# Where a convolution keeps its running sum, who splits the gate weights, and when its layer norm is issued: the last layer of a two-layer diffusion backbone

## The chip, the cores and the metric

The kernel runs on one core of a Trainium2 chip. The metric is the device time of one execution in microseconds (us), as the median of three runs. Five engines with instruction queues of their own work side by side: TensorE (PE: matrix multiplications, written to PSUM), VectorE (DVE), ScalarE (ACT), GpSimd (POOL) and SyncE (SP, which here only issues DMA transfers). Each takes its instructions strictly in the order in which the program was built, and an instruction waits at the head of its queue for what it needs. L1205 is line 1205 of the kernel before; the lines of the changed kernel from L1199 on are one or two higher.

## The reference

Two layers over 512 latent tokens and 256 context tokens of width 1024. Each has a token-mixing part (a convolution branch and an attention branch, merged by gates) and an MLP. The last layer computes only the latent tokens' output; the context gives it just keys and values.

```python
def conformer_conv(u, w_dw, b_dw, ln_g, ln_b):      # u (B, L, 2*512)
    a, g = u[..., :512], u[..., 512:]
    z = a * sigmoid(g)
    z = conv_depthwise(z, w_dw, width=31, pad=15) + b_dw      # per channel, along the tokens
    return silu(layernorm(z, ln_g, ln_b))

def merge_branches(conv_in, attn, gate_logits, ...):
    y_conv = conformer_conv(conv_in, ...) @ w_conv_out        # 512 -> 1024
    y_attn = attn @ w_attn_out                                # 1024 -> 1024
    g = sigmoid(gate_logits + b_gate)                         # 2 * 1024
    return (g[..., :1024] * y_conv + g[..., 1024:] * y_attn) @ w_out

# layer:  p = modulate(rmsnorm(x)) @ w_in    (columns: conv | q | k | v | gates)
#         x = x + gate1 * merge_branches(p_conv, diff_attention(q, k, v), p_gates, ...)
#         x = x + gate2 * sqrelu_mlp(modulate(rmsnorm(x)), w1, w2)
```

## The kernel before

**Three-pass products.** Activations lie with channels on the 128 partitions and tokens along the free axis. A float32 factor is split into a high part, rounded on ACT (L76), and a low part, the remainder, by one subtraction on DVE or POOL (L80). `fm_block` then adds three matmuls for each 128x128 piece of weight and 512 tokens: high times high (L142), low activation times high weight (L143), high activation times low weight (L144). A block of 128 output columns over 1024 input channels is 24 such matmuls. `h_x`, `l_x` and `r_x` are the high part, low part and raw load of weight `x`; `h1h`, `h1l` those of the layer's input, and later, in the same buffers, those of the attention output.

**Stages of the last layer.** The eight attention heads run with projections beside them as filler, the last of them the convolution's input (`z`, L749). Then, in the order of the program:

- The **gate loop**: eight slabs of 256 columns, tiles `gt`, first the four of the attention gates (`half` 1, tiles `g_1_0` to `g_1_7`), then the four of the convolution gates (`half` 0). `gate_slab(half, s, engine)` loads and splits a slab; the low part goes to DVE where no engine is given. Of the 16 `gt` blocks each is 24 matmuls and a sigmoid on ACT (L1257). Slab (1,0) is loaded early and has its low part on POOL; (1,1) is loaded just ahead of the loop, on DVE.
- `spill_rstd`, called in the loop at slab (1,2): the attention heads' normalizing factors `rsall` take a power on POOL (L1028), are transposed on PE (`rsT`, L1058), copied (L1060) and written to memory. From there `branch_load` fetches attention output `ar` and factors `arb` for each head and multiplies them on DVE (L1232); eight heads, four of them loaded ahead.
- The **attention output**: eight blocks `ya`, two for each of four slabs of `w_attn_out`. It needs the splits `h1h`, `h1l` of all eight heads. DVE multiplies each finished block into its gate (`g`, L1335). `ya` has two PSUM banks ("mm"), so a block may start only when that product has read the block two before it.
- The **convolution output**: eight blocks `yc` over four channel tiles, from `ch` and `cl`, the high and low part of the convolution's result; then merge, output projection, second norm and MLP.

**The convolution** is a generator, `taps`: four channel tiles of 128x512, 31 taps each, one DVE instruction for each tap. The first (L1201) starts the sum with the bias, the others (L1205) multiply a shifted view of `z` by a per-channel weight and add the running sum, which lies in SBUF (`ca`, shown as `cacc`). The gate loop and the attention output draw on the generator by `some_taps(n)`: six taps after each of 16 gate blocks, seven after each `ya` block of the first two slabs; what is left is drained ahead of the layer norm.

**The layer norm** of the convolution is a generator of three parts, advanced by `next(ln, None)`. Part 1: the sum `tot` of the four channel tiles on DVE (L1276), a matmul with ones that gives all partitions the mean (`ln`, L1279), four subtractions on DVE (L1283), four squares on ACT and three additions on DVE (`vs`, L1290). Part 2: four small matmuls of `vs`, the reciprocal root on DVE and POOL (`ms_cv`, L354 and L355), its diagonal `dg_cv` (L361). Part 3: a matmul that spreads it over the partitions (L365), then scale (L1308), sigmoid and product (L1312) on DVE and ACT, which give `ch` and `cl`.

**Order.** A scheduler sets each engine's order when the program is built, by priorities that follow the program's order and by its own estimates; the queues are fixed from then on. PSUM has eight banks. In this stage two are "mm" (`gt` and `ya` alternate in them), four "mi" (`ln`, `rsT` and the like), and two "mc", which `ps_for` uses for the context tokens alone, so that the last layer leaves them empty.

Of the kernel before, what the change touches and what calls it, by code (L numbers as in the profile page):

```python
# [8 lines left out]
F32 = mybir.dt.float32  # L9
F32R = mybir.dt.float32r  # L10
AF = mybir.ActivationFunctionType
ALU = mybir.AluOpType
AX = mybir.AxisListType

P = 128
# [11 lines left out]
TAPS = 31  # L27
# [24 lines left out]
def trunk_kernel(  # L52
# [6 lines left out]
    nc = tc.nc  # L59
# [77 lines left out]
    def rows(src, col0, ncols):  # L137
        return src[:, col0 : col0 + ncols].rearrange("(k p) n -> p k n", p=P)
# [318 lines left out]
    for s in range(2):  # L457
        nc.vector.tensor_tensor(
            out=cvec[:, :, s], in0=L["cols"][:, R_C + 8 * s : R_C + 8 * s + 8],
            in1=sg[:, 8 * s : 8 * s + 8], op=ALU.mult)  # L460
# [224 lines left out]
    for i in range(DEPTH):  # L685
        last = i == DEPTH - 1
# [21 lines left out]
        zt = [None] * CT  # L708
# [48 lines left out]
        def gate_slab(half, s, lo_eng=None):  # L757
            wg[half, s] = load_slab(rows(wi, G_OFF + half * D + 256 * s, 256),
                                    f"wg{i}_{half}_{s}", lo_eng=lo_eng)
# [304 lines left out]
        def drain(gen):  # L1064
            for _ in gen:
                pass
# [110 lines left out]
        mc = mcp.__enter__()  # L1177
# [9 lines left out]
        def g3(name, dt=F32):  # L1187
            return gp.tile([P, NT], dt, tag="g3", name=name, bufs=16)
# [3 lines left out]
        CV = nv if last else SEQ + PAD + CTX  # L1192
        CA = qp.tile([P, CT, CV], F32, tag="qk", name=f"cacc{i}")
        ca = [CA[:, cc] for cc in range(CT)]

        def taps():
            for cc in range(CT):
                for t in range(TAPS):
                    wcol = wdc[:, t * CT + cc : t * CT + cc + 1]  # L1199
                    if t == 0:  # L1200
                        nc.vector.tensor_scalar(ca[cc][:, :CV], zt[cc][:, 0:CV], wcol,  # L1201
                                                cols[:, R_BDW + cc : R_BDW + cc + 1],
                                                ALU.mult, ALU.add)
                    else:
                        nc.vector.scalar_tensor_tensor(  # L1205
                            out=ca[cc][:, :CV], in0=zt[cc][:, t : t + CV], scalar=wcol,
                            in1=ca[cc][:, :CV], op0=ALU.mult, op1=ALU.add)
                    yield

        tap = taps()  # L1210

        per_gate, per_ya = (6, 7) if last else (7, 6)

        def some_taps(n):
            for _ in range(n):
# [22 lines left out]
        for half, lst in ((1, ga), (0, gc)):  # L1238
            for s in range(4):
                if (half, s) not in wg:  # L1240
                    gate_slab(half, s)
                if (half, s) == (1, 2):
                    drain(spill_rstd())
                if half == 0 and s == 3:
                    for hg in branch[:4]:
                        branch_load(*hg)
                w = wg.pop((half, s))
                for m in range(2):
                    mb = 2 * s + m
                    t = g3(f"g{i}_{half}_{mb}")  # L1250
                    lst[mb] = t
                    for g in groups:
                        W = g.stop - g.start
                        ps = ps_for(g, f"gt{i}_{half}_{mb}_{g.start}")
                        fm_block(ps[:, :W], w, m * P, lambda k: (hh[:, k], hl[:, k]), g)
                        bcol = R_BG + half * KT + mb
                        nc.scalar.activation(out=t[:, g], in_=ps[:, :W], func=AF.Sigmoid,  # L1257
                                             bias=cols[:, bcol : bcol + 1])
                    some_taps(per_gate)
                    if m == 0 and not state.get("ada_done"):  # L1260
                        ada_slab(i, L, 8 + 4 * half + s)
# [63 lines left out]
        for s in range(4):  # L1325
            w = load_slab(rows(w_attn_out[i], 256 * s, 256), f"wao{i}_{s}")
            if not state.get("ada_done"):
                ada_slab(i, L, 16 + s)
            for g in groups:
                W = g.stop - g.start  # L1330
                for m in range(2):
                    mb = 2 * s + m
                    ps = ps_for(g, f"ya{i}_{mb}_{g.start}")
                    fm_block(ps[:, :W], w, m * P, lambda k: (ah[:, k], al[:, k]), g)
                    nc.vector.tensor_tensor(out=ga[mb][:, g], in0=ga[mb][:, g], in1=ps[:, :W],  # L1335
                                            op=ALU.mult)
                    if last and (s, m) == (3, 0):
                        next(ln, None)
                if s < 1 + last:
                    some_taps(per_ya)  # L1340
            if s == last:
                drain(tap)
                ln = layer_norm()
            if s >= last:
                next(ln, None)


        CL = hpool.tile([P, KT, NT], F32R, tag="hl", name=f"cl{i}")
        for cc in range(CT):
            for a0, W, t0 in cgr:  # L1350
                low = nc.vector.tensor_tensor(out=CL[:, cc, t0 : t0 + W],
                                              in0=ca[cc][:, a0 : a0 + W],
                                              in1=f32(CH[:, cc, t0 : t0 + W]), op=ALU.subtract)
        normed.append(low.ins)
        mh, ml = [None] * KT, [None] * KT
        for s in range(2):
# [7 lines left out]
            for m in range(4):  # L1364
# [9 lines left out]
                for g in groups:  # L1374
                    rr[g.start] = gp.tile([P, 512], F32, tag="ar", bufs=3,
                                          name=f"mr{i}_{mb}_{g.start}")[:, : g.stop - g.start]
# [650 lines left out]
```

## Time and profile before

| | |
|---|---|
| median of 3 runs | 2313.78 us (2309.47 to 2314.64) |
| the profiled execution | 2309.04 us, its span 2307.3 us |
| PE busy | 2234.8 us, 97% of the span, 14402 matmuls |
| DVE busy | 1679.5 us, 73%, 2759 instructions |
| ACT busy | 1056.3 us, 46% |
| POOL busy | 625.9 us, 27%, 774 instructions |
| TensorE clock granted, mean | 0.993 |
| gate loop ends, attention output begins (PE) | 1836.5 us |
| last tap of the last layer's convolution begins (DVE) | 1852.0 us |
| first `yc` block begins (PE) | 1889.5 us |

A row of the timeline reads: start in us, duration, engine, line, operation, output and inputs by the program's names, shapes, count, and in brackets how long the engine was idle just before and what ended that. Rows of groups read: line, engine, operation, forms and count, then busy us, mean ns of one, and idle us before them. Rows of windows give for each stretch its length, the busy us of PE, of the weight loads, of DVE, ACT and POOL (with instructions), the granted clock, the DMA share and GB/s.

### The profile page before, as it was taken

What the parts mean: (1) busy time and instruction counts of PE and PEld (TensorE: products, weight loads), DVE (VectorE), ACT (ScalarE), POOL (GpSimd) and SP (SyncE); (2) the same over time, 40 slices, a digit from 0 to 9 for tenths busy, and PEclk for the clock granted to TensorE, in tenths of its full rate; (3) what the DMA queues carried; (4) which work ended last, traced back from release to release, by engine and by line L of the source; (5) the groups of instructions that cost most, each with busy time, mean ns of one, the idle gap of its engine ahead of it and who ended that gap; (6) DMA issues with size and microseconds to landing.
All of it is one profiled execution on the core that took longest, in us unless ns stands there. A gap on an engine that the chain in (4) does not pass through costs nothing.

```text
span 2307.3 us, 36445 instructions
## 1 busy us (share of the span) xinstructions
PE 2234.8 (97%) x14402; PEld 2021.1 (88%) x14402; DVE 1679.5 (73%) x2759; ACT 1056.3 (46%) x2049; POOL 625.9 (27%) x774
## 2 busy tenths in 40 slices
PE   8999999999999999999999998999999999999999
PEld 6999998888888989998899998999877779888887
DVE  6777776599657678787786567776849966757673
ACT  5555655422323264343346345555642333654541
POOL 1966765110000021222222256766611000100000
PEclk9999999999999999999999999999999999999999
DMA  9211111134444611333345422111114423443151
GB/s 310 62 35 45 47 47 45 44 124 151 148 140 152 203 50 52 105 110 100 128 133 164 141 71 58 44 45 44 43 62 144 130 76 112 154 128 99 66 183 37
DMA packets 202267, 232.63 MB, mean 101 GB/s; under 512 B 8864, under 2 KB 162928, under 8 KB 201968
## 3 DMA queue, kind: packets, MB, share of 16 engines
q1 hardware_dynamic: 202096, 230.30, 31.2%
q8 instruction: 113, 1.85, 0.3%
q14 instruction: 58, 0.48, 0.1%
HBM read 212.93 MB, written 17.35 MB: 100 GB/s over the span
## 4 chain that ended last, share of the span: by engine, by line
PE 75%; DVE 10%; POOL 5%; ACT 4%; DMA 3%; issue 2%; SPq 0%; DVEq 0%; POOLq 0%; ACTq 0%
PE r L151 4%; PE f L143 3%; PE f L144 3%; PE f L142 3%; PE r L143 3%; PE r L142 3%; PE r L144 3%; PE gt L142 3%; PE gt L143 3%; PE gt L144 3%; PE qk L142 2%; PE qk L143 2%; PE qk L144 2%; PE r L154 2%; PE yc L151 2%
## 5 line engine op out<-in xcount | busy, mean ns | idle before, releaser
L1205 DVE SCALAR_TENSOR_TENSOR cacc<-z,cols,cacc 128x783 f32<-128x783 f32 (+1 forms) x240 | 208.6, 929 | 0.3
L142 PE MATMUL qk<-h_wqk,h1h 128*128 128x256 f32 x640 | 182.6, 287 | 2.3 <-ACT rw L797 1.5
L143 PE MATMUL qk<-l_wqk,h1h 128*128 128x256 f32 x640 | 180.2, 284 | 0.0
L969 DVE TENSOR_REDUCE st<-S 128x1 f32<-128x768 f32 (+1 forms) x160 | 134.6, 846 | 57.6 <-PE S L967 56.3
L144 PE MATMUL qk<-h_wqk,h1l 128*128 128x256 f32 x640 | 176.4, 284 | 0.0
L972 ACT ACTIVATE e<-S,st 128x768 f32<-128x768 f32 (+1 forms) x160 | 131.2, 823 | 40.1 <-DVE st L969 39.8
L143 PE MATMUL f<-h2hl,h_w 128*128 128x512 f32 (+1 forms) x416 | 144.0, 347 | 1.2 <-POOL h2hl L80 1.1
L142 PE MATMUL f<-h2hh,h_w 128*128 128x512 f32 (+1 forms) x416 | 142.4, 348 | 2.1 <-ACT h2hh L387 1.1
L144 PE MATMUL f<-h2hh,l_w 128*128 128x512 f32 (+1 forms) x416 | 143.1, 345 | 0.0
L142 PE MATMUL gt<-h1h,h_wg 128*128 128x512 f32 (+1 forms) x384 | 138.1, 360 | 0.0
L143 PE MATMUL gt<-h1l,h_wg 128*128 128x512 f32 (+1 forms) x384 | 136.7, 356 | 0.0
L144 PE MATMUL gt<-h1h,l_wg 128*128 128x512 f32 (+1 forms) x384 | 136.5, 356 | 0.0
L151 PE MATMUL r<-F,whir 128*128 128x512 f32 (+1 forms) x384 | 124.8, 340 | 2.2 <-ACT F L1655 1.9
L142 PEld LDWEIGHTS qk<-h_wqk,h1h 128*128 128x128 f32 x640 | 122.2, 191 | 4.5 <-ACT rw L797 1.7
L151 PE MATMUL r<-F,wlor 128*128 128x512 f32 (+1 forms) x384 | 124.8, 340 | 0.5 <-POOL wlor L1573 0.2
L143 PEld LDWEIGHTS qk<-l_wqk,h1h 128*128 128x128 f32 x640 | 122.2, 191 | 0.3 <-POOL l_wqk L80 0.3
L144 PEld LDWEIGHTS qk<-h_wqk,h1l 128*128 128x128 f32 x640 | 119.9, 191 | 0.3 <-POOL h1l L80 0.2
L142 PE MATMUL v<-h_wv,h1h 128*128 128x256 f32 x384 | 112.2, 292 | 6.5 <-ACT rwc L861 4.0
L324 DVE SCALAR_TENSOR_TENSOR adaac<-ar,cvec,adaac 128x512 f32<-128x512 f32 x105 | 94.5, 919 | 30.7 <-DMA ar<-in_w_ada_dram 30.6
L144 PE MATMUL v<-h_wv,h1l 128*128 128x256 f32 x384 | 109.9, 286 | 0.0
L143 PE MATMUL v<-l_wv,h1h 128*128 128x256 f32 x384 | 109.3, 285 | 0.0
L803 POOL TENSOR_TENSOR rqk<-rqk,mhalf 128x4 f32<-128x4 f32 x80 | 85.8, 1075 | 78.7 <-DVE rqk L802 77.5
(400 smaller groups left out, 7453.5 us busy)
## 6 DMA issues: line engine op xcount, KB each, us to landing
r_w<-in_w_mlp_dram SPq DMA_DIRECT2D x34, 1024.0 KB, 5.4
ada<-in_w_ada_dram SPq DMA_DIRECT2D x24, 1024.0 KB, 5.4
ar<-in_w_ada_dram SPq DMA_DIRECT2D x96, 256.0 KB, 3.3
r_wg<-in_w_in_dram SPq DMA_DIRECT2D x16, 1024.0 KB, 5.2
r_wqk<-in_w_in_dram SPq DMA_DIRECT2D x30, 512.0 KB, 5.1
rf<-in_w_mlp_dram SPq DMA_DIRECT2D x26, 512.0 KB, 3.9
rr<-in_w_mlp_dram SPq DMA_DIRECT2D x24, 512.0 KB, 3.7
r_wao<-in_w_attn_out_dram SPq DMA_DIRECT2D x8, 1024.0 KB, 5.2
```

Source lines behind the costliest of these rows:

```text
L142: nc.tensor.matmul(ps, sh, mh, start=first, stop=False)
L143: nc.tensor.matmul(ps, sh, ml, start=False, stop=False)
L144: nc.tensor.matmul(ps, sl, mh, start=False, stop=last)
L151: nc.tensor.matmul(ps, w[j][:, k, m0 : m0 + P], a(k)[0][:, toks], start=k + j == 0, stop=False)
L154: nc.tensor.matmul(ps, w[0][:, k, m0 : m0 + P], a(k)[1][:, toks], start=False, stop=k == nk - 1)
L324: nc.vector.scalar_tensor_tensor(out=a, in0=r, scalar=cvec[:, k, q : q + 1], in1=a, op0=ALU.mult, op1=ALU.add)
L803: nc.gpsimd.tensor_tensor(out=r, in0=r, in1=mhalf[:, :4], op=ALU.pow)
L969: nc.vector.tensor_reduce(out=st[:, m : m + 1], in_=S[:, :nkey], axis=AX.X, op=ALU.max, negate=True)
L972: nc.scalar.activation(out=e[:, :nkey], in_=S[:, :nkey], func=AF.Exp, bias=st[:, m : m + 1], accum_out=st[:, 2 + m : 3 + m])
L1205: nc.vector.scalar_tensor_tensor(out=ca[cc][:, :CV], in0=zt[cc][:, t : t + CV], scalar=wcol, in1=ca[cc][:, :CV], op0=ALU.mult, op1=ALU.add)
```

## The change

It alters the last layer alone, in three ways.

1. **The running sum** of taps 0 to 29 is a PSUM bank of the "mc" pool (`crun`, two banks for four channel tiles); the 31st tap reads it and writes `ca` in SBUF. The number of taps and their shape are the same.
2. **The low parts** of the six gate slabs that the loop itself loads, (1,2), (1,3) and (0,0) to (0,3), go to POOL instead of DVE: twelve subtractions of 128x1024.
3. **The schedule**: seven taps after each gate block instead of six, taps beside the first `ya` slab only, what is left drained after slab 0 instead of slab 1. The layer norm's three parts are advanced after slabs 0, 1 and 2; before, after slab 1, after slab 2, and in the middle of slab 3.

```diff
@@ -1195,21 +1195,23 @@
 
         def taps():
             for cc in range(CT):
+                run = mc.tile([P, CV], F32, tag="mc", name=f"crun{i}_{cc}") if last else ca[cc]
                 for t in range(TAPS):
                     wcol = wdc[:, t * CT + cc : t * CT + cc + 1]
                     if t == 0:
-                        nc.vector.tensor_scalar(ca[cc][:, :CV], zt[cc][:, 0:CV], wcol,
+                        nc.vector.tensor_scalar(run[:, :CV], zt[cc][:, 0:CV], wcol,
                                                 cols[:, R_BDW + cc : R_BDW + cc + 1],
                                                 ALU.mult, ALU.add)
                     else:
                         nc.vector.scalar_tensor_tensor(
-                            out=ca[cc][:, :CV], in0=zt[cc][:, t : t + CV], scalar=wcol,
-                            in1=ca[cc][:, :CV], op0=ALU.mult, op1=ALU.add)
+                            out=(run if t < TAPS - 1 else ca[cc])[:, :CV],
+                            in0=zt[cc][:, t : t + CV], scalar=wcol,
+                            in1=run[:, :CV], op0=ALU.mult, op1=ALU.add)
                     yield
 
         tap = taps()
 
-        per_gate, per_ya = (6, 7) if last else (7, 6)
+        per_gate, per_ya = 7, 6
 
         def some_taps(n):
             for _ in range(n):
@@ -1238,7 +1240,7 @@
         for half, lst in ((1, ga), (0, gc)):
             for s in range(4):
                 if (half, s) not in wg:
-                    gate_slab(half, s)
+                    gate_slab(half, s, nc.gpsimd if last else None)
                 if (half, s) == (1, 2):
                     drain(spill_rstd())
                 if half == 0 and s == 3:
@@ -1334,15 +1336,12 @@
                     fm_block(ps[:, :W], w, m * P, lambda k: (ah[:, k], al[:, k]), g)
                     nc.vector.tensor_tensor(out=ga[mb][:, g], in0=ga[mb][:, g], in1=ps[:, :W],
                                             op=ALU.mult)
-                    if last and (s, m) == (3, 0):
-                        next(ln, None)
-                if s < 1 + last:
+                if s < 1:
                     some_taps(per_ya)
-            if s == last:
+            if s == 0:
                 drain(tap)
                 ln = layer_norm()
-            if s >= last:
-                next(ln, None)
+            next(ln, None)
 
 
         CL = hpool.tile([P, KT, NT], F32R, tag="hl", name=f"cl{i}")
```

Three places show how the engines' orders move. Names carry buffer numbers; what stands in brackets is the engine or queue that the instruction waits for.

DVE at the end of the gate loop and the start of the attention output, before:

```order
L80 TENSOR_TENSOR l_wg_0_2_19498<-r_wg_0_2_19495,h_wg_0_2_19497 128x1024 [waits Activation_49]
L1205 SCALAR_TENSOR_TENSOR cacc_19061<-z_18576,cols_8470,cacc_19061 128x512 [waits DVE_49] x11
L80 TENSOR_TENSOR l_wg_0_3_19572<-r_wg_0_3_19569,h_wg_0_3_19571 128x1024 [waits DMAHW2_49,PE_49,Activation_49]
L1205 SCALAR_TENSOR_TENSOR cacc_19061<-z_18576,cols_8470,cacc_19061 128x512 [waits DVE_49]
L80 TENSOR_TENSOR l_wg_0_3_19572<-r_wg_0_3_19569,h_wg_0_3_19571 128x1024 [waits Activation_49]
L1205 SCALAR_TENSOR_TENSOR cacc_19061<-z_18576,cols_8470,cacc_19061 128x512 [waits DVE_49] x10
L80 TENSOR_TENSOR l_wao_0_19703<-r_wao_0_19700,h_wao_0_19702 128x1024 [waits DMAHW3_49,PE_49,Activation_49]
L1205 SCALAR_TENSOR_TENSOR cacc_19061<-z_18576,cols_8470,cacc_19061 128x512 [waits DVE_49]
L80 TENSOR_TENSOR l_wao_0_19703<-r_wao_0_19700,h_wao_0_19702 128x1024 [waits Activation_49]
L1205 SCALAR_TENSOR_TENSOR cacc_19061<-z_18576,cols_8470,cacc_19061 128x512 [waits DVE_49] x3
L80 TENSOR_TENSOR h1l_13564<-ar_0_0_19577,h1h_13563 128x512 [waits Activation_49]
```

and after:

```order
L1206 SCALAR_TENSOR_TENSOR crun_2_19398<-z_18576,cols_8470,crun_2_19398 128x512 [waits DVE_49]
L1206 SCALAR_TENSOR_TENSOR crun_3_19581<-z_18576,cols_8470,crun_3_19581 128x512 [waits DVE_49]
L1206 SCALAR_TENSOR_TENSOR cacc_19061<-z_18576,cols_8470,crun_2_19398 128x512 [waits DVE_49]
L1206 SCALAR_TENSOR_TENSOR crun_3_19581<-z_18576,cols_8470,crun_3_19581 128x512 [waits DVE_49]
L80 TENSOR_TENSOR l_wao_0_19723<-r_wao_0_19720,h_wao_0_19722 128x1024 [waits DMAHW3_49,PE_49,Activation_49]
L1206 SCALAR_TENSOR_TENSOR cacc_19061<-z_18576,cols_8470,crun_3_19581 128x512 [waits DVE_49]
L80 TENSOR_TENSOR l_wao_0_19723<-r_wao_0_19720,h_wao_0_19722 128x1024 [waits Activation_49]
L80 TENSOR_TENSOR h1l_13564<-ar_0_0_19595,h1h_13563 128x512 [waits Activation_49]
L80 TENSOR_TENSOR h1l_13564<-ar_1_0_19600,h1h_13563 128x512 [waits Activation_49]
L80 TENSOR_TENSOR h1l_13564<-ar_2_0_19605,h1h_13563 128x512 [waits Activation_49]
```

The subtractions of the gate slab (`l_wg_0_3`) are gone from DVE, and the last tap, which stood behind the products `g_1_0` and `g_1_1` (next place), now stands ahead of the second half of `l_wao_0`. The subtractions of the five slabs ahead of this one are gone from DVE as well; `l_wg_1_1` stays on DVE, after 28 taps instead of 32.

DVE at the end of the first attention-output slab, before:

```order
L80 TENSOR_TENSOR h1l_13564<-ar_6_0_19686,h1h_13563 128x512 [waits Activation_49]
L1205 SCALAR_TENSOR_TENSOR cacc_19061<-z_18576,cols_8470,cacc_19061 128x512 [waits DVE_49]
L80 TENSOR_TENSOR h1l_13564<-ar_7_0_19693,h1h_13563 128x512 [waits Activation_49]
L1276 TENSOR_TENSOR tot_0_19849<-tot_0_19849,cacc_19061 128x512 [waits DVE_49]
L1205 SCALAR_TENSOR_TENSOR cacc_19061<-z_18576,cols_8470,cacc_19061 128x512 [waits DVE_49] x2
L1335 TENSOR_TENSOR g_1_0_19062<-g_1_0_19062,ya_0_0_19708 128x512 [waits PE_49]
L1335 TENSOR_TENSOR g_1_1_19095<-g_1_1_19095,ya_1_0_19734 128x512 [waits PE_49]
L1205 SCALAR_TENSOR_TENSOR cacc_19061<-z_18576,cols_8470,cacc_19061 128x512 [waits DVE_49]
L80 TENSOR_TENSOR l_wao_2_19872<-r_wao_2_19869,h_wao_2_19871 128x1024 [waits DMAHW5_49,Activation_49]
```

and after:

```order
L80 TENSOR_TENSOR h1l_13564<-ar_5_0_19699,h1h_13563 128x512 [waits Activation_49]
L80 TENSOR_TENSOR h1l_13564<-ar_6_0_19706,h1h_13563 128x512 [waits Activation_49]
L1278 TENSOR_TENSOR tot_0_19793<-tot_0_19793,cacc_19061 128x512 [waits DVE_49]
L80 TENSOR_TENSOR h1l_13564<-ar_7_0_19713,h1h_13563 128x512 [waits Activation_49]
L1285 SCALAR_TENSOR_TENSOR cacc_19061<-ln_0_19792,cacc_19061 128x512 [waits PE_49]
L1285 SCALAR_TENSOR_TENSOR cacc_19061<-ln_0_19792,cacc_19061 128x512 x2
L1285 SCALAR_TENSOR_TENSOR cacc_19061<-ln_0_19792,cacc_19061 128x512 [waits DVE_49]
L1337 TENSOR_TENSOR g_1_0_19062<-g_1_0_19062,ya_0_0_19728 128x512 [waits PE_49]
L1337 TENSOR_TENSOR g_1_1_19097<-g_1_1_19097,ya_1_0_19754 128x512 [waits PE_49]
L80 TENSOR_TENSOR l_wao_2_19888<-r_wao_2_19885,h_wao_2_19887 128x1024 [waits DMAHW5_49,Activation_49]
```

The four subtractions of the mean (L1285), which wait for PE's mean `ln`, now stand ahead of the first two gate products (L1337), which free the PSUM banks of `ya_0` and `ya_1`. Before, they stood behind `g_1_2` and `g_1_3`. On PE the mean's matmul moves with them: from behind the last matmul of `ya_3` to just ahead of the last two matmuls each of `ya_0` and `ya_1`.

PE at the matmul that spreads the reciprocal root (L365), before:

```order
L144 MATMUL ya_7_0_19996<-h1h_13563,l_wao_3_19944 128x512
L142 MATMUL ya_7_0_19996<-h1h_13563,h_wao_3_19943 128x512
L365 MATMUL ln_0_19848<-dg_cv_0_19936,cst 128x512 [waits DVE_49]
L143 MATMUL ya_7_0_19996<-h1l_13564,h_wao_3_19943 128x512
L144 MATMUL ya_7_0_19996<-h1h_13563,l_wao_3_19944 128x512
L142 MATMUL ya_7_0_19996<-h1h_13563,h_wao_3_19943 128x512
```

and after:

```order
L143 MATMUL ya_5_0_19919<-h1l_13564,h_wao_2_19887 128x512
L144 MATMUL ya_5_0_19919<-h1h_13563,l_wao_2_19888 128x512
L365 MATMUL ln_0_19792<-dg_cv_0_19880,cst 128x512 [waits DVE_49]
L142 MATMUL ya_6_0_19974<-h1h_13563,h_wao_3_19968 128x512 [waits DVE_49,Activation_49]
L143 MATMUL ya_6_0_19974<-h1l_13564,h_wao_3_19968 128x512
L144 MATMUL ya_6_0_19974<-h1h_13563,l_wao_3_19969 128x512
```

It stood inside `ya_7`, the last block, eight matmuls ahead of `yc_0`; now it stands at the end of `ya_5`, 40 matmuls earlier. Further back on PE, the two small matmuls `av_7_1` now stand four matmuls ahead of the transpose `rsT` instead of one. On SP the loads of the last four gate slabs and of the first two slabs of `w_attn_out`, which waited for DVE to release their buffers, now wait for POOL. Layer 0 and all that follows the convolution output keep their order.

## Prediction

> **What bounds the kernel.** I read the page first: how busy each engine is, and the chain that ended last.
>
> ```profile
> PE 2234.8 (97%) x14402; PEld 2021.1 (88%) x14402; DVE 1679.5 (73%) x2759; ACT 1056.3 (46%) x2049; POOL 625.9 (27%) x774
> PE 75%; DVE 10%; POOL 5%; ACT 4%; DMA 3%; issue 2%; SPq 0%; DVEq 0%; POOLq 0%; ACTq 0%
> ```
>
> TensorE is the bound, and the change leaves its matmuls as they are. DVE time that it saves is therefore worth nothing by itself: only the moments count in which PE stands still in this part of the last layer. So next the windows of the stretch from 1756 to 1893 us. Columns: length, then busy us of PE, weight loads, DVE, ACT and POOL, then granted clock, DMA share, GB/s.
>
> ```profile
> 1756.14:1759.55 3.41, 0.94 (x5) 0.81 (x6) 3.41 (x5) 0.22 (x1) 2.42 (x1) 1.00 0.00 0
> 1759.55:1762.96 3.41, 3.41 (x10) 2.63 (x9) 3.41 (x7) 0.69 (x1) 0.00 (x0) 0.50 0.55 163
> 1760.00:1836.00 76.00, 76.00 (x330) 62.79 (x330) 74.18 (x104) 25.40 (x32) 0.00 (x0) 0.98 0.51 167
> 1836.00:1852.00 16.00, 12.71 (x54) 9.48 (x53) 15.96 (x25) 6.88 (x9) 0.00 (x0) 1.00 0.41 130
> 1852.00:1887.00 35.00, 35.00 (x155) 28.15 (x154) 18.58 (x29) 7.14 (x11) 1.01 (x1) 1.00 0.28 90
> 1885.84:1889.25 3.41, 1.35 (x6) 0.76 (x5) 3.41 (x6) 2.48 (x4) 0.00 (x0) 1.00 0.00 0
> 1889.25:1892.67 3.42, 3.17 (x8) 2.50 (x9) 3.42 (x7) 2.75 (x6) 0.00 (x0) 0.50 0.00 0
> ```
>
> PE has three gaps: ahead of 1759, in the first attention-output slab (1836 to 1852), and ahead of `yc`. Between them it never stops. The 35 us with 155 matmuls give its pitch, 35.00 / 155 = 0.226 us. Two gaps cost more than their length: where PE was busy for only 0.94 and 1.35 of 3.41 us, the clock granted in the next window is 0.50, and half of 3.41 us is **1.7 us** lost on top. The slab's gap has no such dip behind it.
>
> **What ends the gaps**, from PE's timeline, with the idle time in brackets:
>
> ```profile
> 1758.61 0.29 PE L1058 MATMUL rsT<-cst,rsall 128*32 128x128 f32 x1 [3.00 <-POOL rsall L1028]
> 1836.31 0.39 PE L144 MATMUL gt<-h1h,l_wg 128*128 128x512 f32 x1
> 1843.85 0.50 PE L143 MATMUL ya<-h1l,h_wao 128*128 128x512 f32 x1 [1.24 <-DVE h1l L80]
> 1846.32 0.50 PE L143 MATMUL ya<-h1l,h_wao 128*128 128x512 f32 x1 [0.81 <-DVE h1l L80]
> 1851.50 0.50 PE L142 MATMUL ya<-h1h,h_wao 128*128 128x512 f32 x1 [1.24 <-DVE g L1335]
> 1862.52 1.02 PE L1279 MATMUL ln<-tot,cst 128*128 128x512 f32 x2
> 1884.33 1.02 PE L365 MATMUL ln<-dg_cv,cst 128*128 128x512 f32 x2
> 1889.50 0.80 PE L151 MATMUL yc<-ch,h_wco 128*128 128x512 f32 x1 [2.30 <-ACT ch L1314]
> 1897.31 0.50 PE L151 MATMUL yc<-ch,h_wco 128*128 128x512 f32 x1 [0.54 <-DVE g L1371]
> ```
>
> The first slab of `ya` took 1851.50 - (1836.31 + 0.23) = 15.0 us for 48 matmuls worth 48 x 0.226 = 10.8: **4.1 us** lost.
>
> **Term 1, the transpose `rsT`.** PE waited 3.00 us for one tiny POOL operation, and paid a dip of 1.7. Of its kind there are these:
>
> ```profile
> 1725.73 0.73 POOL L1028 TENSOR_TENSOR rsall<-rsall,mhalf 128x2 f32<-128x2 f32 x1 [2.45 <-ACT rsall L1025]
> 1755.86 2.69 POOL L1028 TENSOR_TENSOR rsall<-rsall,mhalf 128x2 f32<-128x2 f32 x1 [12.13 <-ACT rsall L1025]
> 1738.58 5.70 DVE L1205 SCALAR_TENSOR_TENSOR cacc<-z,cols,cacc 128x512 f32<-128x512 f32 x2
> 1737.93 5.81 POOL L80 TENSOR_TENSOR l_wg<-r_wg,h_wg 128x1024 fp32r<-128x1024 f32 x2 [11.47 <-ACT h_wg L76]
> 1787.90 7.39 DVE L1205 SCALAR_TENSOR_TENSOR cacc<-z,cols,cacc 128x512 f32<-128x512 f32 x11
> L80 DVE TENSOR_TENSOR wtl<-wT,wth x144: 411/557/560, 100.6 to 1747.3; 128x384 fp32r<-128x384 f32 x128, 128x256 fp32r<-128x256 f32 x16
> L821 DVE TENSOR_TENSOR dup<-ra,rb x64: 405/426/2618, 65.1 to 1672.2; 128x256 f32<-128x256 f32 x64
> ```
>
> The same 128x2 power takes 0.73 us or 2.69. Two taps take 5.70 us beside POOL's `l_wg`, but eleven take 7.39 without it, 0.67 each. So DVE and POOL stop each other. The last two rows (minimum, median, maximum ns) say when: `wtl` reads one of its inputs from PSUM and never exceeds 560 ns in 144 instructions through the heads, where POOL works too; `dup` reads both from SBUF and goes from 426 to 2618. A tap reads `z` and its sum; with the sum in PSUM it becomes like `wtl`. This is the step on which the change rests. [...]
>
> Then the power takes 0.73 us instead of 2.69. The two matmuls ahead of it on PE stand three `gt` matmuls earlier, 0.7 us. The wait falls from 3.00 to about 3.00 - 1.96 - 0.4 (only part of the 0.7 reaches it, through ACT) = 0.6, which brings no dip: gain 2.4 + 1.7 = **4.1 us**. Bounds: 2, if the power still meets a half of `l_wg_1_1`, which stays on DVE, or its copy; 4.7, if nothing is left.
>
> **Term 2, the taps and the low parts.** DVE gives up twelve halves of a gate slab, POOL takes them:
>
> ```profile
> 1728.52 0.69 DVE L749 TENSOR_TENSOR z<-z,sg 128x512 f32<-128x512 f32 x1 [1.35 <-ACT sg L746]
> L80 DVE TENSOR_TENSOR l_wg<-r_wg,h_wg 128x1024 fp32r<-128x1024 f32 x14 | 17.2, 1228 | 0.0
> L80 POOL TENSOR_TENSOR l_wqk<-r_wqk,h_wqk x18: 2363/2408/3381, 18.5 to 1628.1; 128x1024 fp32r<-128x1024 f32 x18
> 1803.87 2.01 ACT L76 ACTIVATE h_wg<-r_wg 128x1024 fp32r<-128x1024 f32 x2 [4.52 <-PE gt L143]
> L1205 DVE SCALAR_TENSOR_TENSOR cacc<-z,cols,cacc 128x512 f32<-128x512 f32 x120 | 87.3, 790 | 0.1
> L1232 DVE TENSOR_TENSOR ar<-ar,arb 128x512 f32<-128x512 f32 x8 | 5.5, 692 | 0.2 <-DMA arb<-rs_d 0.2
> ```
>
> For POOL: a slab's high part starts when PE begins the slab before it and takes 2.01; two halves of 2.4 to 2.9 follow the first high half, so the low part is ready 1.0 + 5.8 = 7 us into the 10.9 us (48 x 0.226) of that slab. Four are to spare, and the loads that now wait for POOL have them too: hidden, at no cost. Were POOL's halves stretched by half, that cover would be gone and PE would wait about 2 us at each of six slabs.
>
> For DVE: twelve times 1.14 (the group's 1.228 with the overlap of neighbours off, an estimate) are 13.7 us less, and the 5.70 - 1.34 = 4.4 us of the stalled pair go too. From the first `z` at 1728.5 the convolution then needs 124 x 0.66 = 82 us, some 7 for `z`, `wtl`, `l_wg_1_1` and the small copies, 2.8 for four `ar`, and perhaps 9 for waits and for the `ar`, which read SBUF twice and can still meet POOL: it ends near 1829, 7 us ahead of the gate loop's end, where before the last tap began at 1852.0. In the profile before, DVE was 74.18 of 76 us busy in the loop, so this room is real.
>
> No DVE instruction of the kernel before writes PSUM, so the price of such a tap isn't shown. Nearest rows:
>
> ```profile
> L1308 DVE SCALAR_TENSOR_TENSOR cacc<-cacc,cols,ln 128x512 f32<-128x512 f32 x4 | 2.7, 744 | 3.8 <-PE ln L365 3.8
> L1312 DVE SCALAR_TENSOR_TENSOR cacc<-cacc,cols,cs 128x512 f32<-128x512 f32 x4 | 2.9, 748 | 0.0
> L1283 DVE SCALAR_TENSOR_TENSOR cacc<-ln,cacc 128x512 f32<-128x512 f32 x4 | 2.5, 684 | 0.2 <-PE ln L1279 0.2
> ```
>
> The same operation with one input in PSUM takes 744 against 748 ns from SBUF, and 684 with the shorter form: reading PSUM costs nothing. For writing I take nothing either, with 744 - 684 = 60 ns either way as bounds: 120 x 0.06 = 7 us of DVE. Downward it is worth nothing more; upward the conv ends at the loop's end, and the splits `h1l` come late (the first rival). [...]
>
> **Term 3, the first `ya` slab.** The taps between its splits are gone, but on DVE three `ar`, two `tot`, both halves of `l_wao_1` and `ar_7` stand ahead of `h1l_4`: 4 x 0.69 + 2 x 0.65 + 2 x 1.2 = 6.5 us from the landing of `ar_4`. Reading back from 1843.85 through the old order (6 us), `ar_4` was there near 1837. So `h1l_4` ends near 1844.4, and PE wants it 26 matmuls into the slab, 1836.5 + 5.9 = 1842.4: wait **2.0** (0.8 if `ar_4` is fetched earlier, as its buffer comes free when `h1l_0` is done; 2.4 if not at all). The later splits follow at 0.7 us, PE uses one in 1.4.
>
> Then comes a new wait. The block `ya_2` needs the bank of `ya_0`, so the product `g_1_0`; this now stands behind four subtractions, and they wait for the mean.
>
> ```profile
> 1863.58 2.48 DVE L1283 SCALAR_TENSOR_TENSOR cacc<-ln,cacc 128x512 f32<-128x512 f32 x4 [0.17 <-PE ln L1279]
> 1850.76 1.28 DVE L1335 TENSOR_TENSOR g<-g,ya 128x512 f32<-128x512 f32 x2
> ```
>
> If `ln` starts at t, the subtractions start at t + 1.06 (1863.58 - 1862.52), end at t + 3.5, `g_1_0` ends at t + 4.2 and `ya_2` starts at t + 4.3. PE has `ln` (0.9) and four matmuls (0.9) to do until t + 1.8: it waits **2.5 us**. Queued behind on DVE are `g_1_1` and `l_wao_2`, wanted 10.9 us later. Sum 2.0 + 2.5 = 4.5 against 4.1 before. An idle stretch of 2.5 us leaves 0.9 busy if it falls into one window, like the 0.94 that brought a dip; I count the dip, 1.7. **Loss 0.4 + 1.7 = 2.1 us.** Bounds: a gain of 1 (wait 0.8 and no dip), a loss of 5 (both waits 2.4 or more, and two dips).
>
> **Term 4, the start of `yc`.** Before, the matmul L365 started at 1884.33 and `yc` at 1889.50, 5.2 us later, which is the chain from it to the first `ch`. Now it stands at the end of `ya_5`, with 48 matmuls or 10.9 us behind it: the chain is covered by `ya_6` and `ya_7`, also the later `ch`, which follow at some 1.5 us. Its input is in time, as parts 1 and 2 of the norm have slabs 1 and 2 (10.9 us each) for themselves. Gone are 2.30, 0.54 and the dip of 1.7: **gain 4.5 us** (3 to 5). If the cover failed, the old 4.5 would return.
>
> **Sum.** 4.1 - 2.1 + 4.5 = 6.5 us. The profiled execution becomes 2309.04 - 6.5 = 2302.5. The median of the runs, 2313.78, is 4.7 above that execution; the same gain off the median is **2307.3**.
>
> **Rivals.**
>
> *The PSUM sum is dearer to write* (0.15). For it: it is not shown. Against: reads are free. From 30 ns a tap the slack of 7 us is half used and the splits slip; at 60 ns the conv ends at the loop's end, `ar_4` and `h1l` come some 6 us later, PE waits for them, and the 6.5 are gone: about 2314.
>
> *The new wait takes more than I count* (0.25). Two dips, and a power that still meets `l_wg_1_1`: term 1 at 2, term 3 at -4, term 4 at 4.5, 2.5 us in all: 2311.
>
> *Slower: the PSUM sum does not free DVE from POOL* (0.10). Then each of twelve POOL halves holds DVE for its 2.4 us less a tap's own time, as in the stalled pair (4.4 us for two halves, 2.2 each): 26 us more, 13.7 less for the halves. With my 7 us of slack used and no 13.7 credited twice (the 1829 has it already), the conv ends 1829 + 26 = 1855, 19 us past the loop's end, and all of it stands ahead of `h1l` in DVE's order: about 2307.3 + 20 to 26, say 2331. It decides from four blocked halves on. Against it: `wtl`, 144 times.
>
> *The change does not do what it says* (0.02): PSUM banks clash, or POOL's low parts come late and PE waits at the slabs: 2316 to 2325.
>
> **How the numbers follow.** The forecast has 0.48, with 2303 to 2309.5 as its own range. What a measurement of this kernel can tell from no change is about 0.2%, 4.6 us. Faster by more than that (below 2309.2): the forecast and a little of the second rival, 0.50. Slower (above 2318.4): the third rival, half the last, a bad case of the first, 0.14. The rest, 0.36, is within 0.2%. The range from 2302 to 2316 leaves out the slower cases and a few better ones.
>
> **What would show it.** In the changed profile: taps of 0.66 to 0.68 us beside POOL's `l_wg`; the power near 0.73; PE's gap at `rsT` under 1 us without a half clock behind it; the last tap ahead of the gate loop's end; a new gap of 2 to 3 us ahead of `ya_2`, released by `g`; no gap ahead of `yc`. It is wrong if taps beside POOL take over a microsecond, if the last tap falls behind the gate loop, or if the gap at `ya_2` is missing.

## The result

The changed kernel takes **2303.89 us** (median of 11 runs, 2300.27 to 2307.82) against 2312.14 of the kernel before in the same comparison (11 runs, 2304.91 to 2314.64): ratio **0.9967**, 95% interval 0.9958 to 0.9976. By the ratio that is 7.6 us; the medians lie 8.2 apart. Run once more, beside other kernels, it gave 0.9964 (0.9950 to 0.9977). Forecast were 2307.3 us and a gain of 6.5. One execution of the new schedule alone, among the experiments, took 5610.67 us; it was disturbed and is in no ratio.

The page after, beside the first line quoted of before: PE has the same matmuls, DVE 17 us less, POOL 29 more.

```profile
PE 2232.1 (97%) x14402; PEld 2018.7 (88%) x14402; DVE 1662.5 (72%) x2747; ACT 1053.5 (46%) x2049; POOL 654.9 (28%) x786
```

PE's timeline of the changed kernel, at the places of the gaps of before, with the spreading matmul L365:

```profile
1752.72 0.29 PE L1058 MATMUL rsT<-cst,rsall 128*32 128x128 f32 x1 [0.32 <-POOL rsall L1028]
1837.63 0.58 PE L143 MATMUL ya<-h1l,h_wao 128*128 128x512 f32 x1 [2.14 <-DVE h1l L80]
1847.62 0.50 PE L142 MATMUL ya<-h1h,h_wao 128*128 128x512 f32 x1 [2.24 <-DVE g L1337]
1872.05 1.02 PE L365 MATMUL ln<-dg_cv,cst 128*128 128x512 f32 x2
1883.82 0.40 PE L151 MATMUL yc<-ch,h_wco 128*128 128x512 f32 x1
```

The wait at the transpose is 0.32 us instead of 3.00, the wait ahead of `yc` is gone, and in the first slab two gaps stand, of 2.14 and 2.24 us. The rows that explain them, from POOL's and DVE's timelines and from the groups of DVE and of the tile `crun`:

```profile
1751.97 0.70 POOL L1028 TENSOR_TENSOR rsall<-rsall,mhalf 128x2 f32<-128x2 f32 x1 [12.10 <-ACT rsall L1025]
1797.55 4.78 POOL L80 TENSOR_TENSOR l_wg<-r_wg,h_wg 128x1024 fp32r<-128x1024 f32 x2 [6.10 <-ACT h_wg L76]
1799.58 17.87 DVE L1206 SCALAR_TENSOR_TENSOR crun<-z,cols,crun 128x512 f32<-128x512 f32 x27
1820.41 0.74 DVE L1206 SCALAR_TENSOR_TENSOR cacc<-z,cols,crun 128x512 f32<-128x512 f32 x1
1825.14 2.73 DVE L80 TENSOR_TENSOR h1l<-ar,h1h 128x512 fp32r<-128x512 f32 x4 [2.85 <-ACT h1h L76]
L1206 DVE SCALAR_TENSOR_TENSOR crun<-z,cols,crun x116: 733/750/751, 1727.5 to 1818.0; 128x512 f32<-128x512 f32 x116
L1202 DVE TENSOR_SCALAR crun<-z,cols x4: 806/808/812, 1726.1 to 1779.8; 128x512 f32<-128x512 f32 x4
```

A tap on the PSUM sum never takes more than 751 ns, in 116 instructions. 27 of them run at 17.87 / 27 = 0.66 us beside POOL's `l_wg`, which itself takes 4.78 for two halves. The last tap ends at 1821.1, 7.9 us ahead of the gate loop's end at 1829.0.

**By stages.** PE's work in this part falls into three stages: from the first `gt` matmul to the first `ya`, from there to the last `ya`, from there to the last `yc` (starts of matmuls in PE's timeline). What follows, up to DVE's last instruction, takes 386.8 to 386.9 us in the profile before, the one after and the repeated one alike. The sums are rounded from unrounded stages.

| us | gate loop | attention output | convolution output | sum |
|---|---|---|---|---|
| before | 93.5 | 50.3 | 29.5 | 173.4 |
| changed, first profile | 89.3 | 54.6 | 25.2 | 169.0 |
| changed, repeated (first experiment) | 89.3 | 51.4 | 25.2 | 165.9 |

So the change takes 4.3 us from the first stage and 4.3 from the last, and gives back between 1.1 and 4.3 in the middle: 7.5 or 4.3 in all. The profiled executions differ by 8.7 us (2309.04 and 2300.37). Of these, 3.2 lie ahead of the gate loop, where the kernels are alike and the execution before had two half-clock windows more (seven against five), 4.3 in the three stages, and 1.1 behind DVE's last instruction, where the output is written. Ahead of the loop these windows number from five to eleven in the profiles of this study, so one pair of whole executions settles no difference of 3 us; the stages do.

### The profile page after: what moved, and what is told of

It reads as the page before. It is cut to its first block, busy times and chain, and to the rows that moved or that the text cites. A ratio compares the mean times of both kernels' runs of the same rounds, so it can differ in the third digit from the quotient of the medians.

```text
span 2298.6 us, 36455 instructions
## 1 busy us (share of the span) xinstructions
PE 2232.1 (97%) x14402; PEld 2018.7 (88%) x14402; DVE 1662.5 (72%) x2747; ACT 1053.5 (46%) x2049; POOL 654.9 (28%) x786
## 4 chain that ended last, share of the span: by engine, by line
PE 78%; DVE 8%; POOL 5%; ACT 4%; DMA 3%; issue 2%; SPq 0%; DVEq 0%; POOLq 0%; ACTq 0%
PE r L151 5%; PE f L143 3%; PE f L144 3%; PE f L142 3%; PE r L143 3%; PE r L142 3%; PE r L144 3%; PE gt L142 3%; PE gt L144 3%; PE gt L143 3%; PE r L154 2%; PE qk L142 2%; PE qk L143 2%; PE qk L144 2%; PE o L142 2%
## 5 line engine op out<-in xcount | busy, mean ns | idle before, releaser
L1206 DVE SCALAR_TENSOR_TENSOR cacc<-z,cols,cacc 128x783 f32<-128x783 f32 x120 | 121.1, 1060 | 0.2
```

The source lines that it names most:

```text
L1206: nc.vector.scalar_tensor_tensor(out=(run if t < TAPS - 1 else ca[cc])[:, :CV], in0=zt[cc][:, t : t + CV], scalar=wcol, in1=run[:, :CV], o ...
```

## The experiments

| | gate loop | attention output | convolution output | ratio to before (95%) |
|---|---|---|---|---|
| changed, repeated | 89.3 | 51.4 | 25.2 | 0.9964 (0.9950 to 0.9977) |
| products first | 89.3 | 48.3 | 25.2 | 0.9951 (0.9938 to 0.9965) |
| products first, six loads | 89.3 | 46.2 | 25.2 | 0.9943 (0.9931 to 0.9956) |
| PSUM sum, POOL's low parts, old schedule | 89.3 | 50.9 | 27.6 | 0.9980 (0.9971 to 0.9989) |
| POOL's low parts, new schedule, sum in SBUF | 123.6 | 46.4 | 25.2 | 1.0095 (1.0075 to 1.0115) |
| PSUM sum alone | 89.3 | 50.2 | 29.6 | 0.9983 (0.9974 to 0.9992) |
| new schedule alone | 93.6 | 50.3 | 26.3 | 0.9987 (0.9977 to 0.9997) |

### The changed kernel again

> The changed kernel unaltered, as the yardstick for the three beside it. The time was 2303.89 us (0.9967 of before). Its profile showed two gaps in the first attention-output slab (2.14 us ahead of h1l_4, 2.24 ahead of ya_2), each with a half clock in the window behind it. If the dips follow from gaps of that length, they are there again, at most one of them missing where a gap falls across two windows; if they were chance, a second profile shows them elsewhere. Expected 2302 to 2306 us.

Both gaps are there, without a half clock behind either: the expectation held for the gaps, and "at most one missing" was wrong. The time, 2301.63 us, fell just below the expected 2302 to 2306. The windows show where the two executions differ. In each of the nine profiles all half-clock windows start within 4 ns of one grid with a step of 3.413 us (in the profile before and the first one after, all single ones but the last are recorded as 3413 ns long), so that the clock's windows can be counted on through an execution from any of them. The stretches shown here lie within 0.06 us of that grid. First the two windows with the gaps and those behind them in the first profile, then the three windows around the gaps in the repeated one:

```profile
1834.46:1837.87 3.41, 1.27 (x6) 0.76 (x5) 3.41 (x6) 0.63 (x1) 0.00 (x0) 1.00 0.20 65
1837.87:1841.28 3.41, 3.41 (x9) 2.65 (x9) 2.11 (x4) 0.00 (x0) 0.00 (x0) 0.51 0.69 243
1844.70:1848.11 3.41, 1.17 (x5) 0.65 (x5) 3.41 (x7) 2.87 (x4) 0.00 (x0) 1.00 0.00 0
1848.11:1851.52 3.41, 3.41 (x10) 2.67 (x9) 3.31 (x5) 1.21 (x3) 0.00 (x0) 0.51 0.04 1
```

```profile
1841.51:1844.93 3.42, 2.02 (x9) 1.38 (x8) 3.42 (x6) 0.63 (x1) 0.00 (x0) 1.00 0.32 88
1848.34:1851.76 3.42, 2.28 (x9) 1.19 (x7) 2.03 (x4) 1.28 (x2) 0.00 (x0) 1.00 0.00 0
1851.76:1855.17 3.41, 2.31 (x10) 1.90 (x11) 3.41 (x5) 2.81 (x5) 0.00 (x0) 1.00 0.00 0
```

```profile
1844.41 0.50 PE L143 MATMUL ya<-h1l,h_wao 128*128 128x512 f32 x1 [1.40 <-DVE h1l L80]
1852.86 0.50 PE L142 MATMUL ya<-h1h,h_wao 128*128 128x512 f32 x1 [2.24 <-DVE g L1337]
```

The same 2.24 us lay within one window the first time (PE busy 1.17 of 3.41, then clock 0.51). The second time it fell across the border near 1851.8, about 1.1 us on either side: PE was busy 2.28 and 2.31, and the clock stayed. In these two executions the gap cost its length, and 1.7 us on top in the one where it lay within one window.

### The products ahead of the subtractions

```diff
                     dd = ca[cc][:, a0 : a0 + W]
-                    nc.vector.scalar_tensor_tensor(out=dd, in0=mu[:, :W], scalar=-1.0 / CW, in1=dd,
-                                                   op0=ALU.mult, op1=ALU.add)
+                    with ExitStack() as behind:
+                        for ins in freed:
+                            behind.enter_context(tc.issue_after(ins))
+                        nc.vector.scalar_tensor_tensor(out=dd, in0=mu[:, :W], scalar=-1.0 / CW,
+                                                       in1=dd, op0=ALU.mult, op1=ALU.add)
 ... (further down, `prod` is the gate product g)
+                    if last and s == 0:
+                        freed.append(prod.ins)
```

> The changed kernel, with the four subtractions of the mean issued on DVE behind the gate products g_1_0 and g_1_1 instead of ahead of them; nothing else moves. Theory (the new wait of term 3): the gap ahead of ya_2 falls from 2.24 us to between 0.5 and 1.3, the half clock behind it goes (1.7 us), and the time falls by about 2.5 to 3.3 us against the changed kernel, to near 2301. Rival (the slab is late anyway, the product only shows where): the gap stays or moves to the next block, within 1 us of the changed kernel.

```profile
1844.26 0.50 PE L143 MATMUL ya<-h1l,h_wao 128*128 128x512 f32 x1 [0.97 <-DVE h1l L80]
1850.75 0.50 PE L142 MATMUL ya<-h1h,h_wao 128*128 128x512 f32 x1 [0.32 <-DVE g L1341]
```

The gap ahead of `ya_2` falls from 2.24 to 0.32 us, further than expected, and none comes in its place. The stage takes 48.3 us instead of 51.4 or 54.6. The times alone would not part theory from rival: the medians are 2300.15 and 2301.63, 1.5 us apart, and the intervals of the ratios overlap. The timeline does. The new wait of term 3 is shown: it was the place in DVE's queue. The wait for `h1l_4` also came out shorter, 0.97 instead of 1.40, which this edit doesn't touch, so not all of the 3.1 us are the edit's.

### Six attention-output buffers instead of four

```diff
-            r = gp.tile([P, 512], F32, tag="t2k", bufs=4, ...
+            r = gp.tile([P, 512], F32, tag="t2k", bufs=6 if last else 4, ...
 ...
-                    for hg in branch[:4]:
+                    for hg in branch[: 6 if last else 4]:
```

The edit of the run before is in it too, and the norm's `vs`, which shares these buffers, has six as well.

> As the run before, and the attention output has six buffers instead of four, so that heads 4 and 5 are fetched ahead of the gate loop's end instead of after the split of head 0. Theory: the wait for h1l_4 (2.14 us) is set by that fetch, not by the convolution, which had ended 8 us ahead; gap and half clock go, 2.1 + 1.7 us more: near 2297.5, 0.9935 of before. Rival: DVE's own work ahead of the split (sums, l_wao_1) sets it, and then at most 1 us is gained; near 2300.

PE's timeline marks no gap any more from 1834 to 1884, and the stage takes 46.2 us; the same work at PE's pitch of 0.226 us, 192 matmuls and two for the norm, is about 45 (an estimate). The time is 2298.25 us, near the theory's 2297.5 and not far below the rival's 2300, but the stage decides: 2.1 us less with the gap of 0.97 gone, and the splits ready earlier. DVE's timeline shows how:

```profile
1833.29 2.49 DVE L80 TENSOR_TENSOR h1l<-ar,h1h 128x512 fp32r<-128x512 f32 x4
1835.85 1.32 DVE L1234 TENSOR_TENSOR ar<-ar,arb 128x512 f32<-128x512 f32 x2
```

Six splits (two of them just ahead, at 1831.5) are done by 1835.8, one microsecond into the slab, with `ar_4` and `ar_5` among them. Of the three its median is the lowest. Against the repeated changed kernel the stage is 5.2 us shorter (51.4 to 46.2) and the median 3.4 (2301.63 to 2298.25); medians hold half clocks at other places too.

### The old schedule on the new resources

```diff
-        per_gate, per_ya = 7, 6
+        per_gate, per_ya = (6, 7) if last else (7, 6)
 ... the layer norm's parts after slabs 1 and 2 and in the middle of slab 3, as before
```

> The changed kernel with the schedule of before (six taps after each gate block, layer norm's parts advanced after slabs 1 and 2 and in slab 3); PSUM sum and POOL's low parts stay. The scheduler still moves the mean to the first slab, so that both gaps there stay; only the spreading matmul L365 returns to ya_7, 14 matmuls ahead of yc instead of 48. Theory: PE is free 4.1 us after that matmul starts and the first ch needs 5.2, so yc waits 1.1 us without a half clock: 1 to 2 us slower than the changed kernel, near 2305.5. Rival (term 4 as predicted belongs to this edit): the whole 4.5 us return, near 2308.4.

2306.24 us, 0.9980: between theory and rival, nearer the theory. PE waits 0.94 us for the first `ch`, but the products and later `ch` cost more than I counted:

```profile
1887.21 0.50 PE L151 MATMUL yc<-ch,h_wco 128*128 128x512 f32 x1 [0.94 <-ACT ch L1316]
1888.35 0.50 PE L151 MATMUL yc<-ch,h_wco 128*128 128x512 f32 x1 [0.40 <-ACT ch L1316]
1894.41 0.50 PE L151 MATMUL yc<-ch,h_wco 128*128 128x512 f32 x1 [0.73 <-DVE g L1373]
```

The last stage takes 27.6 us instead of 25.2, and both gaps of the first slab stay (1.47 and 2.24), without a half clock. So about half of the 4.3 us of the last stage is the schedule's, 2.4; the other 2 come with the two resources alone, as the scheduler then moves the norm forward by itself. The window that holds most of the gap of 2.24 had PE busy for less than half of it, and the clock of the next one stayed at 1.00:

```profile
1847.72:1851.14 3.42, 1.53 (x6) 0.76 (x4) 2.78 (x5) 2.03 (x3) 0.00 (x0) 1.00 0.00 0
1851.14:1854.55 3.41, 3.06 (x13) 2.55 (x14) 3.41 (x5) 2.06 (x4) 0.00 (x0) 1.00 0.00 0
```

### The sum back in SBUF

```diff
-                run = mc.tile([P, CV], F32, tag="mc", name=f"crun{i}_{cc}") if last else ca[cc]
+                run = ca[cc]
```

> The changed kernel with the running sum back in SBUF: POOL's low parts and the new schedule stay. Theory (two SBUF inputs stop DVE while POOL reads): each of POOL's twelve halves costs DVE about 2.2 us, 26 us in all, so that the last tap ends near 1847 us in the changed kernel's profile time instead of 1821; the splits h1l stand behind it, PE waits some 15 to 20 us at the first attention-output slab, and the time is 2318 to 2326 us; the two-column power takes over 2 us again. Rival (PSUM buys nothing, relief of DVE does it all): within 3 us of the changed kernel.

2333.55 us, ratio 1.0095: slower, as the theory had it, and still further than its range. But it is not DVE that pays, and not at the attention output. The groups of `l_wg` on POOL (minimum, median, maximum ns), DVE's taps beside them, and PE:

```profile
L80 POOL TENSOR_TENSOR l_wg<-r_wg,h_wg x14: 2364/2832/27875, 1742.7 to 1852.7; 128x1024 fp32r<-128x1024 f32 x14
1771.14 12.46 POOL L80 TENSOR_TENSOR l_wg<-r_wg,h_wg 128x1024 fp32r<-128x1024 f32 x1 [7.74 <-ACT h_wg L76]
1767.42 13.98 DVE L1206 SCALAR_TENSOR_TENSOR cacc<-z,cols,cacc 128x512 f32<-128x512 f32 x21
1819.30 36.24 POOL L80 TENSOR_TENSOR l_wg<-r_wg,h_wg 128x1024 fp32r<-128x1024 f32 x4 [5.36 <-ACT h_wg L76]
1802.03 51.25 DVE L1206 SCALAR_TENSOR_TENSOR cacc<-z,cols,cacc 128x512 f32<-128x512 f32 x58
1760.68 2.72 POOL L1028 TENSOR_TENSOR rsall<-rsall,mhalf 128x2 f32<-128x2 f32 x1 [12.11 <-ACT rsall L1025]
1763.46 0.28 PE L1058 MATMUL rsT<-cst,rsall 128*32 128x128 f32 x1 [3.02 <-POOL rsall L1028]
1783.66 0.79 PE L144 MATMUL gt<-h1h,l_wg 128*128 128x512 f32 x1 [6.91 <-POOL l_wg L80]
1847.23 0.79 PE L144 MATMUL gt<-h1h,l_wg 128*128 128x512 f32 x1 [17.60 <-POOL l_wg L80]
```

Two of the twelve halves were held up beside DVE's taps, one right behind the other. The first took 12.46 us and ended 2.2 us after DVE's row of 21 taps had (1781.40); the second lasted 27.9 us instead of 2.4, and 38 taps ran past it at full pace. What let that one in, and why the other ten took only 2.4 to 4.0 us, the rows don't show. DVE lost 51.25 - 58 x 0.66 = 13 us in the second row, PE 17.6, waiting for the weights' low part. The gate loop took 34 us longer than in the changed kernel: 6.91 + 17.60, the transpose's 2.7, and 6.9 for the 13.9 us that PE was busy in half-clock windows make 34. In the attention output PE had no gap, and the stage took 46.4 us. So POOL's low parts are only to be had here with the sum in PSUM: with the sum in SBUF they cost about 25 us (1.0095 against the 0.9987 of the new schedule alone, below).

### The PSUM sum alone

```diff
-                    gate_slab(half, s, nc.gpsimd if last else None)
+                    gate_slab(half, s)
 ... and the old schedule
```

> The kernel before with the PSUM sum alone: gate low parts on DVE, schedule of before. (With the new schedule and DVE low parts, every engine's order comes out the same as this.) Theory: the power falls to 0.7 us and the gap at the transpose with its half clock goes, 4.2 us; the gap ahead of yc stays with its half clock; in the first slab the old gaps stay within 1 us. Near 2307.5 us. Rival (POOL's low parts, not the PSUM sum, relieve the transpose): the gap at the transpose stays at 3 us; within 1 us of before.

2306.13 us, 0.9983: the theory, stage by stage. The power and the gap at the transpose are as in the changed kernel, the gap ahead of `yc` as before:

```profile
1757.88 0.70 POOL L1028 TENSOR_TENSOR rsall<-rsall,mhalf 128x2 f32<-128x2 f32 x1 [12.10 <-ACT rsall L1025]
1758.64 0.28 PE L1058 MATMUL rsT<-cst,rsall 128*32 128x128 f32 x1 [0.32 <-POOL rsall L1028]
1887.80 0.50 PE L151 MATMUL yc<-ch,h_wco 128*128 128x512 f32 x1 [2.30 <-ACT ch L1316]
```

The whole 4.3 us of the first stage belong to the PSUM sum. POOL's low parts add nothing to that stage, nor, with the old schedule, to the time beyond doubt (0.9980 against 0.9983). They end the convolution early: 5.9 us ahead of the gate loop's end with the old schedule, where without them, here, it ends 20.9 behind. How far the new schedule needs that is open; the next experiment has it without.

### The new schedule alone

```diff
-                run = mc.tile(...) if last else ca[cc]
+                run = ca[cc]
-                    gate_slab(half, s, nc.gpsimd if last else None)
+                    gate_slab(half, s)
```

> The kernel before with the new schedule alone: sum in SBUF, low parts on DVE. The spreading matmul stands 25 matmuls (5.6 us) ahead of yc, whose first ch needs 5.2 us: the gap ahead of yc goes with its half clock, 4 to 4.5 us; the gap at the transpose stays (3.0 and 1.7 us); in the first slab the mean comes behind the products as before, gaps within 1 us of before. Near 2308. Rival (the chain isn't ready so early, since the convolution ends as late as before): a new gap at the mean or at the spreading matmul takes the gain; within 1.5 us of before.

2306.39 us, 0.9987: a gain of about 3 us, less than 4 to 4.5. For its profile it ran once more:

> The new schedule alone once more, for its profile. By the stages of the other profiles: the gate loop takes 93.5 us as before (transpose and its half clock unrelieved), the yc stage 25.2 instead of 29.6 if the matmul L365, moved 17 matmuls earlier, covers the chain; the attention output then pays for it, since the timed runs gave 0.9987, 3 us, and not the 4.4 of yc: about 1 to 1.5 us more than 50.3. If it is the yc gap that stays in part, its stage takes 26.5 to 28 us and the attention output 50.3.

```profile
1762.64 0.28 PE L1058 MATMUL rsT<-cst,rsall 128*32 128x128 f32 x1 [3.00 <-POOL rsall L1028]
1855.53 0.50 PE L142 MATMUL ya<-h1h,h_wao 128*128 128x512 f32 x1 [1.26 <-DVE g L1337]
1893.15 0.50 PE L151 MATMUL yc<-ch,h_wco 128*128 128x512 f32 x1 [0.47 <-DVE g L1337]
1898.10 0.51 PE L151 MATMUL yc<-ch,h_wco 128*128 128x512 f32 x1 [0.55 <-DVE g L1370]
```

Neither branch of that expectation hit whole: gate loop 93.6 and attention output 50.3 as before, `yc` 26.3, with 1.0 us left of its gaps and no half clock. 3.2 us of gain by the stages, which is what the timed runs gave. This one execution took 2308.82 us beside 2308.57 of one of the kernel before, so it shows no gain as a whole; it had eleven half-clock windows ahead of the loop. The mean's subtractions stand behind the products here, as before, and the new wait doesn't arise.

## Why the prediction was right, step by step

| step | predicted | measured | shown by |
|---|---|---|---|
| term 1, transpose | +4.1 us | +4.3 | stage 1; PSUM sum alone |
| term 2, a tap that writes PSUM | nothing, or 60 ns either way | 750 ns against 754 in the kernel before (medians) | `crun`, 116 taps |
| term 2, end of the convolution | 7 us ahead of the loop's end | 7.9, repeated 5.9 | DVE's timeline |
| term 3, wait for `h1l_4` | 2.0 us | 2.14 and 1.40 | PE's timeline |
| term 3, wait at `ya_2` | 2.5 us, one half clock | 2.24; half clocks two and none | products first |
| term 3, sum | -2.1 us | -4.3 and -1.1 | stage 2 |
| term 4, start of `yc` | +4.5 us | +4.3 | stage 3 |

**The forecast's way of going was right**, and its sum of 6.5 us lies between the two profiles' 4.3 and 7.5 and below the runs' 7.6. The absolute time, 2307.3, was 3.4 us too high, and 1.6 of that come from where it was counted: the median of before, 2313.78 in three runs, is 2312.14 in eleven. The step that was mis-sized is term 3: not its waits, but the half clock, which I counted once, as if by rule. There are two in one execution and none in another of the same program, nor in the old schedule's, which has both gaps. How often they come wasn't measured; that the forecast's one lies between the two cases is partly luck.

Term 3 also left open what sets the wait for `h1l_4`. The first split, `h1l_0`, starts 3.9 us ahead of the first `ya` matmul in all eight profiles with four buffers, whether the convolution has ended by then or, as before, runs on for 16 us behind the loop; its early end can't help the splits. In the first profile DVE stands idle for 2.85 us until ACT's `h1h` lets `h1l_0` go. That buffer holds the layer's input until the last `gt` block has read it (argued from the program; the row shows only the wait). Past that point the fetch of `ar_4`, tied to the split of head 0, sets the slab: the wait was 2.14, 1.40, 0.97 and 1.47 us in four profiles, and six buffers took it away.

In term 2 one aside doesn't follow from its own numbers: with POOL's halves stretched by half, the low part would be ready 1.0 + 8.7 = 9.7 us into the 10.9 of a slab, still in time. It would come late only if they doubled. It wasn't put to the test, as two halves took 4.78 us.

**Term 4** was put down to the schedule alone. On top of the new resources the schedule brings 2.4 of the 4.3 us, and the scheduler moves the rest by itself; alone it brings 3.3 (29.5 to 26.3). How the 4.3 divide thus depends on which comes first, and neither brings them all.

**The rivals.** The dearer PSUM tap is refuted for the tap, whose median is 750 ns with the sum in PSUM against 754 with the sum in SBUF. Only the first of each tile is dearer, 808 ns instead of the 543 of its like in the kernel before, 1 us for all four. Of the rival of the larger new wait, the two half clocks came in the first profile and not in the second; its other part, a power on POOL that is still held up, came in neither (0.70 us). The slower rival was built as an experiment by putting the sum back, and its time, 2331, was nearly met (2333.55), but for another reason than I gave: I had DVE pay for POOL's turns and the splits come late; instead one POOL subtraction took 27.9 us beside DVE's taps, and PE waited 17.60 us for it. A number that fits is no proof of its mechanism.

## What to carry to other kernels

Where two engines stop each other, as DVE and POOL do here (two taps with both inputs in SBUF took 5.70 us beside POOL's 5.81), try moving one operand of the long row of instructions to PSUM: here 27 taps then ran at 0.66 us each beside POOL's subtractions, which took 4.78 us for two. Only then try to move work to the other engine: here the second without the first cost about 25 us. When work is issued sooner, look at what stands behind its first waiting instruction; four subtractions ahead of two products cost 2 us here, and putting them in the other order gave it back. Measure small gains by stages between fixed points of the bound engine's timeline, since half-clock windows elsewhere, five to eleven of them ahead of the gate loop at up to 1.7 us each, moved the total by as much as the effect.

## What was not expected

- **A starved POOL instruction.** A subtraction of 2.4 us took 12.5 and 27.9 beside a row of two-SBUF-input taps on DVE. Before, two taps had taken 5.70 beside POOL's 5.81, which looked like an even exchange. The second, which 38 taps ran past, took more than ten times its usual 2.4 us.
- **A clock window with a border.** PE idle for 2.24 us cost 1.7 us more when it fell in one window (busy 1.17 of 3.41, a third, and the next window at 0.51) and nothing when a border near 1851.8 parted it (2.28 and 2.31). How long PE was busy in a window does not settle it by itself: a half-clock window followed a full-clock one with 2.04 us of PE busy, and none followed the 1.53 of the old schedule. These rows, of the run with the sum back in SBUF, show the 2.04 and the half clock behind it; what the clock goes by is not shown:

```profile
829.12:832.53 3.41, 2.04 (x10) 1.23 (x9) 2.79 (x7) 2.30 (x6) 0.60 (x1) 1.00 0.00 0
832.53:835.94 3.41, 3.06 (x14) 3.06 (x15) 2.91 (x7) 3.28 (x9) 1.76 (x3) 0.50 0.00 0
```
